# Expert gates scattered into DRAM by accumulating DMAs in place of one-hot matmuls

## The chip, the core and the metric

The kernel runs on one NeuronCore of a Trainium2 chip. The metric is the time of one execution on the device in microseconds (us), of which lower is better. Five engines work side by side and wait for one another on semaphores: TensorE (PE in the profile; PEld is its weight loading), VectorE (DVE), ScalarE (ACT), GpSimd (POOL), and SyncE (SP), which here only issues DMAs. ACT and POOL issue DMAs too.

## The reference

A decoder trunk of two layers over 256 tokens of width 1024 in float32. Each layer adds three things to the residual x: a mixer (stick-breaking attention and retention), a cross-attention to a memory, and PEER, a feed-forward part over 16,384 experts of one neuron each. The change is in PEER, which picks 16 experts for each token and head:

```python
def peer_ffn(h, w_pq, sub_keys, expert_u, expert_v):
    q = (h @ w_pq).reshape(B, S, PEER_HEADS, 2, PEER_DQ // 2)       # 8 heads, 2 halves
    scores = jnp.einsum('bshpd,hpkd->bshpk', q, sub_keys)           # 128 keys per half
    top_s, top_i = lax.top_k(scores, K)                             # K = 16
    cand_s = (top_s[..., 0, :, None] + top_s[..., 1, None, :]).reshape(B, S, PEER_HEADS, K * K)
    cand_i = (top_i[..., 0, :, None] * NK + top_i[..., 1, None, :]).reshape(B, S, PEER_HEADS, K * K)
    best_s, best_pos = lax.top_k(cand_s, K)
    expert_idx = jnp.take_along_axis(cand_i, best_pos, axis=-1)
    gate = jax.nn.softmax(best_s, axis=-1)
    ...
        a = jnp.einsum('cd,chkd->chk', hc, u)                       # u, v: rows expert_idx
        w = gc * jax.nn.gelu(a, approximate=False)
        return jnp.einsum('chk,chkd->cd', w, v)
```

The kernel computes this densely: the product of h with all 16,384 rows of expert_u, a gelu, a product with a dense gate matrix G (expert by token, zero where an expert was not picked), and the product with all rows of expert_v.

## The kernel before

All weights stream through SBUF in 680 units of 512 KB in the order of their use (`Stream`, L31 to L69): SP loads a unit into one of three `raw` buffers (L48), ACT rounds it to `hi` (L57), and DVE forms the rest `lo` (L59); three pairs of `hi` and `lo` exist, so that two units are ready ahead of the one that PE works on. SP carries out its list in order, and the load of a unit waits there until the `raw` buffer of three units before is free, that is until its `lo` is done. A unit's product takes three matmuls for each pair of tiles (`hi`·hi, `hi`·lo, `lo`·hi).

A layer has 84 units for mixer, cross-attention and the query projection `pq` (16 of them), 128 for expert_u and 128 for expert_v. Other work is cut into generators that run one step for each unit (`Side`, L87); `paced` (L72) lets the selection of experts spend a fixed cost per unit, its `rate`, where a step's cost is written beside its `yield`.

In PEER, `stage1` (L796) multiplies queries by keys, `top16` (L784) takes the best 16 on DVE in five instructions, `select` (L821) does this once more over the 256 sums of a head and makes gates and expert numbers for 128 tokens, and transposes them. `g_build` (L893) then makes G in SBUF: for four tokens at a time DVE writes one-hot tiles `oh2` and `oh1` in float16 (L907, L911), PE multiplies them in eight matmuls of 128x128 into `gps` (L900), and ACT copies them into `gt` (L901). That takes 64 steps per layer, beside the units of expert_u.

The gelu of an expert_u product is stored to the DRAM tensor `tdr` as long as G is not complete (L946); afterwards it is multiplied into `gt` at once (`ev_u`, L942). In the expert_v part `w_load` (L967) brings stored gelus back, `w_prep` (L973) multiplies them by `gt` and splits the product into `wh` and `wl`, and `v_mm` (L994) accumulates in `out` (L999). The order of expert_v's units puts the direct ones first.

Of the kernel before, what the change touches and what calls it, by code (L numbers as in the profile page):

```python
# [10 lines left out]
F32 = mybir.dt.float32  # L11
# [4 lines left out]
OP = mybir.AluOpType  # L16
# [10 lines left out]
RATE = 1.12, 1.6  # L27
GS = 2.0 ** 14  # keeps the low parts of small gates clear of float16's smallest numbers
# [43 lines left out]
def paced(g, rate):  # L72
    """spreads g over the units, rate[0] of its cost to each; g yields the cost of a step, None to end a unit's share"""
    credit = 0.0
    while True:
        credit += rate[0]
# [38 lines left out]
def build(tc, ctx, a):  # L115
# [9 lines left out]
    v_at = []  # L125
    for l in range(L):
# [11 lines left out]
        v_at.append(len(units))  # L138
        units += [None] * 128
# [10 lines left out]
    cm = const.tile([128, 256 + 16], F32)  # L150
    gains = const.tile([128, L, 40], F32)
    c_sp = ExitStack()
# [12 lines left out]
    iota = cm[:, 128:256]  # L165
    iota16 = cm[:, 256:272]
    mhalf = const.tile([128, 8], F32)
    G.memset(mhalf, -0.5)
    hT = const.tile([128, KT, 512], F32R)
    tdr = dram.tile([64, 128, 512], F32)  # L170
# [47 lines left out]
    def b_pair_halves(src, evac, mid):  # L218
        """the first pair of such tiles, k = 0-3 of both before mid() and k = 4-7"""
# [18 lines left out]
    def b_units(src, n, evac, first=0):  # L238
        """pairs of [128 n, 256 t] = W^T @ src; evac(pair, psum [128, 2, 256])."""
# [20 lines left out]
    def split_g(src, dst, k0, gain, new_ps):  # L260
        """transposes [128 t, 128] pieces src(tt, 0), src(tt, 1), times gain, into dst[:, k0:k0+2] as hi and lo."""
# [10 lines left out]
    def split_gs(srcs, dst, k0, gain, new_ps):  # L272
        """the same of srcs[tt][:, 0:512], a pair per step"""
# [8 lines left out]
    class Norm:  # L282
        """rmsnorm of x: x is transposed at once, in pieces, times the gain; its 1/rms goes onto the products."""
# [35 lines left out]
    def normed_t(src, gain, dst, hn, new_ps):  # L319
        """dst = transposed rmsnorm(src) * gain, hi and lo"""  # L320
# [27 lines left out]
    for l in range(L):  # L348
# [24 lines left out]
        side.add(load_task())  # L373
        ntri, mask, mneg = (cx[:, i * 128:(i + 1) * 128] for i in range(3))
# [379 lines left out]
        c_pe, c_g0, c_top, c_g1, c_ps = (ExitStack() for _ in range(5))  # L754
        pe = pool(c_pe, "pe", 2)
        slot = pe.tile([128, 2, 4, 128], F16, name="slot")
        iota_x = pe.tile([128, 128, 4], F16, name="slot")
        G.tensor_copy(iota_x, iota[:, :, None].to_broadcast([128, 128, 4]))
        gt = {}
# [12 lines left out]
        def h_task():  # L772
            """the normalized hT of the expert products"""
# [18 lines left out]
        queue = [deque(), deque()]  # L792
        qts = deque()

        def stage1(g, qT):
# [3 lines left out]
            s = pw.tile([128, 2, 128], F32, name="s", bufs=14)  # L799
            A.copy(s, ps)  # L800
            for tt in range(2):
                queue[tt].append(lambda tt=tt: top16(s[:, tt], 128, tv[:, tt, g], ti[:, tt, g]))

        def ev_q(i, ps):
            q2 = pw.tile([128, 2, 256], F32, name="q2")
            A.copy(q2, ps)
            for c in range(2):
                qts.append((2 * i + c, q2[:, c]))

        cands = {}  # L810

        def cand(tt, h):
            if h >= PH or (tt, h) in cands:
                return
            cd = pw.tile([128, TOPK, TOPK], F32, name="cd", bufs=3)
            G.tensor_tensor(cd, tv[:, tt, 2 * h][:, :, None].to_broadcast([128, TOPK, TOPK]),
                            tv[:, tt, 2 * h + 1][:, None, :].to_broadcast([128, TOPK, TOPK]), op=OP.add)
            cands[tt, h] = cd

        def select(tt):  # L820
            """best 16 of the 256 sums per head, gates, expert numbers"""  # L821
            bv = keys.tile([128, PH, TOPK], F32, name="bv", bufs=2)
            bp = keys.tile([128, PH, TOPK], U32, name="bp", bufs=2)
            cand(tt, 0)
            cand(tt, 1)
            yield 0
            for h in range(PH):
                cand(tt, h + 2)
                top16(cands[tt, h].rearrange("p a b -> p (a b)"), 256, bv[:, h], bp[:, h])
                yield 1.7  # L830
            gs = keys.tile([128, 4, PH, TOPK], F32, name="gs", bufs=2)
            be = keys.tile([128, PH, TOPK], F32, name="be", bufs=2)
            V.tensor_tensor(be, bv, bv[:, :, 0:1].to_broadcast([128, PH, TOPK]), op=OP.subtract)
            A.activation(be, be, AF.Exp, scale=rx[:, tt:tt + 1])
            pf = keys.tile([128, 2, PH, TOPK], F16, name="pf", bufs=2)
            for w in range(2):
                pi = keys.tile([128, PH, TOPK], U32, name="pi", bufs=2)
                if w == 0:
                    V.tensor_scalar(pi, bp, 4, None, op0=OP.logical_shift_right)
                else:  # L840
                    V.tensor_scalar(pi, bp, 15, None, op0=OP.bitwise_and)
                V.tensor_copy(pf[:, w], pi)
            yield 1.0
            yield None
            s8 = small.tile([128, PH], F32, name="r8")
            V.tensor_reduce(s8, be, axis=AX.X, op=OP.add)
            V.reciprocal(s8, s8)
            V.tensor_scalar(s8, s8, GS, None, op0=OP.mult)
            V.tensor_tensor(be, be, s8[:, :, None].to_broadcast([128, PH, TOPK]), op=OP.mult)
            g16 = keys.tile([128, PH, TOPK], F16, name="g16")  # L850
            V.tensor_copy(g16, be)
            V.tensor_copy(gs[:, 2], g16)
            V.tensor_sub(gs[:, 3], be, gs[:, 2])
            yield 1.2
            tih = ti[:, tt].rearrange("p (h w) c -> p h w c", w=2)
            for w in range(2):
                for hf in range(2):
                    hs = slice(4 * hf, 4 * hf + 4)
                    tx = keys.tile([128, 4, TOPK, TOPK], F16, name="tx", bufs=2)
                    A.copy(tx, tih[:, hs, w][:, :, :, None].to_broadcast([128, 4, TOPK, TOPK]))  # L860
                    eq = keys.tile([128, 4, TOPK, TOPK], F16, name="eq", bufs=2)
                    V.tensor_tensor(eq, iota16x[:, None].to_broadcast([128, 4, TOPK, TOPK]),
                                    pf[:, w, hs, None, :].to_broadcast([128, 4, TOPK, TOPK]), op=OP.is_equal)
                    yield 0.6
                    V.tensor_mul(eq, eq, tx)
                    yield 0.6
                    V.tensor_add(eq[:, :, 0:8], eq[:, :, 0:8], eq[:, :, 8:16])
                    V.tensor_reduce(gs[:, w, hs], eq[:, :, 0:8].rearrange("p h c s -> p h s c"), axis=AX.X, op=OP.add)
                    yield 0.9
            yield None  # L870
            ps = sps.tile([128, 4, 128], F32, name="sps")
            for w in range(4):
                T.transpose(ps[:, w], gs[:, w].rearrange("p h c -> p (h c)"), ident)
            yield None
            A.copy(slot[:, tt], ps)
            yield 0

        def q_task():
            n = 0
            while n < 32:  # L880
                if qts:
                    for _ in range(2):
                        stage1(*qts.popleft())
                qn = queue[0] if len(queue[0]) >= len(queue[1]) or n >= 24 and queue[0] else queue[1]
                if qn:
                    qn.popleft()()
                    n += 1
                    yield 1.05
                else:
                    yield None  # L890

# [241 lines left out]
```

## Time and profile before

| what | value |
|---|---|
| median of 3 runs | 2158.88 us (2157.48 to 2158.95) |
| span of the profiled execution | 2156.0 us |
| PE busy | 2137.1 us, 99% |
| DVE, ACT, POOL busy | 72%, 54%, 4% |
| granted TensorE clock | 0.999 of full speed (2.4 GHz) |
| DMA | 425.72 MB, 197 GB/s mean |

The span is the time from the first instruction to the last of the one execution that was profiled. The profile gives no other time for that execution; the median of the runs lies 2.9 us above its span. Matmuls are pipelined and their durations overlap, so a matmul's mean in nanoseconds is longer than the step from one to the next: the step is read from starts.

### The profile page before, as it was taken

To read this page: it belongs to the slowest core of one execution; us is meant where nothing else is said; L and a number is where in the kernel's file an instruction comes from. 1 tells how busy PE (TensorE), PEld (TensorE's weight loads), DVE (VectorE), ACT (ScalarE), POOL (GpSimd) and SP (SyncE) were. 2 spreads that over 40 slices of the span, in tenths; PEclk is the share of its full clock that TensorE was granted. 3 is DMA by queue.
4 is the path that set the end of the run, shared out by engine and by line. 5 is a ranking of instruction groups with operands and counts; after the bars stand their busy time and mean duration, and the time that the engine had idled before them with its cause. 6 is when DMAs were issued, how large, how long until landed. Compare 5 with 4: busy or idle time off the path is not lost.

```text
span 2156.0 us, 35478 instructions
## 1 busy us (share of the span) xinstructions
PE 2137.1 (99%) x14028; PEld 1955.8 (91%) x14028; DVE 1544.2 (72%) x2583; ACT 1173.0 (54%) x1483; POOL 81.8 (4%) x87
## 2 busy tenths in 40 slices
PE   8999999999999999999999999999999999999998
PEld 7899899999999988888888899999999998888887
DVE  5775699886766567677676747998876755666776
ACT  6645554556665444444466445545666654444444
POOL 0120000000000000000011100000000000000000
PEclk9999999999999999999999999999999999999999
DMA  6544557775555577777755445677755565777775
GB/s 220 157 152 150 160 177 229 232 231 161 157 162 181 185 234 239 242 243 239 233 183 162 142 151 167 184 236 227 219 162 158 162 184 183 240 240 242 244 244 185
DMA packets 133222, 425.72 MB, mean 197 GB/s; under 512 B 14912, under 2 KB 15040, under 8 KB 132800
## 3 DMA queue, kind: packets, MB, share of 16 engines
q1 hardware_dynamic: 114624, 386.98, 56.5%
q10 hardware_dynamic: 18432, 36.50, 5.8%
q8 instruction: 109, 1.79, 0.3%
q14 instruction: 57, 0.47, 0.1%
HBM read 393.53 MB, written 29.88 MB: 196 GB/s over the span
## 4 chain that ended last, share of the span: by engine, by line
PE 67%; issue 31%; ACT 1%; DVE 1%; DMA 0%; POOL 0%; POOLq 0%; ACTq 0%
PE out L999 16%; PE mm L249 11%; PE mm L250 11%; PE mm L252 11%; PE mm L192 4%; PE mm L194 4%; PE mm L193 4%; PE gps L900 3%; PE sps L798 1%; PE att L689 1%; PE att L720 1%; PE att L425 0%; PE tp L265 0%; PE mm L492 0%; PE mm L228 0%
## 5 line engine op out<-in xcount | busy, mean ns | idle before, releaser
L59 DVE TENSOR_TENSOR lo<-raw,hi 128x1024 fp32r<-128x1024 f32 x680 | 834.2, 1229 | 319.0 <-ACT hi L57 315.6
L57 ACT CAST hi<-raw 128x1024 fp32r<-128x1024 f32 x680 | 713.2, 1051 | 448.1 <-PE mm L250 260.0
L249 PE MATMUL mm<-hT,hi 128*128 128x256 f32 x2272 | 561.9, 286 | 0.0
L250 PE MATMUL mm<-hT,hi 128*128 128x256 f32 x2272 | 552.0, 281 | 0.0
L999 PE MATMUL out<-hi,oh 128*128 128x512 f32 x2048 | 548.9, 389 | 0.0
L999 PEld LDWEIGHTS out<-hi,oh 128*128 128x128 f32 x2048 | 384.3, 188 | 79.5
L249 PEld LDWEIGHTS mm<-hT,hi 128*128 128x128 f32 x2272 | 429.8, 189 | 0.4
L250 PEld LDWEIGHTS mm<-hT,hi 128*128 128x128 f32 x2272 | 428.8, 189 | 0.2
L999 PE MATMUL out<-lo,oh 128*128 128x512 f32 x1024 | 316.7, 389 | 0.0
L252 PE MATMUL mm<-hT,lo 128*128 128x256 f32 x2272 | 315.8, 282 | 0.0
L252 PEld LDWEIGHTS mm<-hT,lo 128*128 128x128 f32 x2272 | 289.3, 188 | 0.0
L999 PEld LDWEIGHTS out<-lo,oh 128*128 128x128 f32 x1024 | 192.3, 188 | 39.8
L901 ACT ACTIVATE gt<-gps 128x512 f32<-128x512 f32 x128 | 137.6, 1113 | 83.2 <-PE gps L900 83.2
L907 DVE TENSOR_TENSOR oh<-slot 128x1024 f16<-128x1024 f16 x128 | 88.3, 690 | 107.5 <-PE gps L900 107.5
L900 PE MATMUL gps<-oh,oh 128*128 128x128 f16 x1024 | 137.4, 297 | 0.0
L900 PEld LDWEIGHTS <-oh 128*128 128x128 f16 x1024 | 107.5, 118 | 6.0
L911 DVE TENSOR_TENSOR oh<-oh,slot 128x1024 f16<-128x1024 f16 x128 | 88.3, 690 | 3.3
L192 PE MATMUL mm<-hi,hT 128*128 128x512 f32 x160 | 64.5, 403 | 0.0
L258 POOL TENSOR_TENSOR rstd<-rstd,mhalf 128x2 f32<-128x2 f32 (+1 forms) x8 | 5.5, 684 | 1550.3 <-DVE rstd L298 1550.3
L194 PE MATMUL mm<-lo,hT 128*128 128x512 f32 x160 | 63.2, 395 | 0.0
L193 PE MATMUL mm<-hi,hT 128*128 128x512 f32 x160 | 63.1, 395 | 0.0
L249 PE MATMUL mm<-hTp,hi 128*128 128x256 f32 x224 | 55.5, 286 | 0.0
(728 smaller groups left out, 2184.0 us busy)
## 6 DMA issues: line engine op xcount, KB each, us to landing
raw<-u SPq DMA_DIRECT2D x256, 512.0 KB, 4.0
raw<-v SPq DMA_DIRECT2D x256, 512.0 KB, 3.6
raw<-w_in_a SPq DMA_DIRECT2D x40, 512.0 KB, 3.5
raw<-pq SPq DMA_DIRECT2D x32, 512.0 KB, 3.4
raw<-w_in_b SPq DMA_DIRECT2D x16, 512.0 KB, 4.8
raw<-wkv_b SPq DMA_DIRECT2D x16, 512.0 KB, 3.6
raw<-w_out SPq DMA_DIRECT2D x16, 512.0 KB, 3.5
raw<-wkv_a SPq DMA_DIRECT2D x16, 512.0 KB, 4.0
```

Source lines behind the costliest of these rows:

```text
L57: self.nc.scalar.copy(hi, r)
L59: self.nc.vector.tensor_sub(lo, r, hi.bitcast(F32))
L192: T.matmul(ps[tt], sh, h3[:, kk], start=(k == 0), stop=False)
L193: T.matmul(ps[tt], sl, h3[:, kk], start=False, stop=False)
L194: T.matmul(ps[tt], sh, l3[:, kk], start=False, stop=(k == KT - 1))
L249: T.matmul(o, h3[:, k], src[:, k, 0:256], start=(k == 0), stop=False)
L250: T.matmul(o, h3[:, k], src[:, k, 256:512], start=False, stop=False)
L252: T.matmul(o, l3[:, k], src[:, k, 0:256], start=False, stop=(k == KT - 1))
L900: T.matmul(ps[:, i], a0[:, 1, :, i], b0[:, w, :, i], start=(w == 0), stop=(w == 1))
L901: pend.append(lambda: A.activation(gt[tt][:, :, c0:c0 + 4].rearrange("p i t -> p t i"), ps, AF.Copy, scale=1.0 / GS))
L907: V.tensor_tensor(a1, iota_x[:, None].to_broadcast([128, 2, 128, 4]), slot[:, tt, 0:2, None, c_].to_broadcast([128, 2, 128, 4]), op=OP.is_ ...
L999: T.matmul(out[tt][dd], st_, mv_[:, dd * 512:(dd + 1) * 512], start=(i == 0 and first), stop=(i == 127 and mv_ is lo))
```

## The change

The one-hot tiles, their matmuls, `gt`, `tdr` and the two orders of expert_v go. In their place stands a DRAM tensor `gd` for each layer and half of the tokens, 16,384 x 128 floats. `zero_task` fills it with zeros from SBUF in 64 DMAs of 256 KB per layer, one per weight unit from the fifth on, on SP's queue. The selection runs in four groups of two heads, each for all 256 tokens. `gates` computes for every gate its place in `gd` (expert number times 128 plus token) and adds the gate there with an indirect accumulating DMA from GpSimd's queue, 128 elements of 4 bytes each: 2 halves x 16 ranks x 8 heads = 256 DMAs per layer. The first DMAs of a head wait until those of the head before have landed. The sums of candidates `cd` move from POOL to DVE. Gelus stay in SBUF (`act0`, `act1`). In the expert_v part SP loads the gates of two units (`gw`, 2 DMAs of 128 KB), and DVE multiplies them by `act`; the very first of these loads waits for all scatter DMAs.

```diff
@@ build
-        units += [None] * 128
+        units += [a["v"][l, i] for i in range(128)]
+    zeros = const.tile([128, 128], F32)
+    gd = [[dram.tile([NK * NK * 128, 1], F32, name=f"gd{l}{tt}") for tt in range(2)] for l in range(L)]
@@ layer
+        def zero_task():
+            for tt in range(2):
+                g_ = gd[l][tt].rearrange("(n p q t) o -> n p q (t o)", p=128, q=4, t=128)
+                for n in range(32):
+                    nc.sync.dma_start(g_[n], zeros[:, None].to_broadcast([128, 4, 128]))
+                    yield
+        side.later(zero_task(), 4)
@@ gates, in place of the end of select and g_build
+                    eq = keys.tile(SH4, F16, name="eq", bufs=2)
+                    V.tensor_tensor(eq, iota16x[:, None].to_broadcast(SH4),
+                                    pf[:, w, tt, :, None, :].to_broadcast(SH4), op=OP.is_equal)
+                    V.tensor_mul(eq, eq, tx[w][tt])
...
-                        T.matmul(ps[:, i], a0[:, 1, :, i], b0[:, w, :, i], start=(w == 0), stop=(w == 1))
-                pend.append(lambda: A.activation(gt[tt][:, :, c0:c0 + 4].rearrange("p i t -> p t i"), ps,
-                                                 AF.Copy, scale=1.0 / GS))
...
+            V.tensor_scalar(gi, ex[:, 0], 128.0, pcol, op0=OP.mult, op1=OP.add)
+            for h in range(HG):
+                now = [[], []]
+                for c in range(TOPK):
+                    for tt in range(2):
+                        i_ = G.indirect_dma_start(
+                            gd[l][tt], bass.IndirectOffsetOnAxis(ap=gi[:, tt, h, c:c + 1], axis=0),
+                            gv[:, tt, h, c:c + 1], None, compute_op=OP.add).ins
+                        for j_ in now[tt]:
+                            tc.declare_no_dep(i_, j_, reason="one head's experts differ")
+                        if c == 0:
+                            for j_ in late[tt]:
+                                tc.add_manual_dep(i_, j_.name, SYNC, reason="the sums of an earlier head")
+                        now[tt].append(i_)
+                late[:] = now
@@ peer_task: four groups; costs 1.6 and 2.6, rate 1.6
+                    for tt in range(2):
+                        top16(sc[k][:, tt], 128, tv[:, tt, k], ti[:, tt, k])
+                        yield 1.6
...
+                        V.tensor_tensor(cd, tv[:, tt, 2 * h][:, :, None].to_broadcast([128, TOPK, TOPK]),
+                                        tv[:, tt, 2 * h + 1][:, None, :].to_broadcast([128, TOPK, TOPK]), op=OP.add)
+                        top16(cd.rearrange("p a b -> p (a b)"), 256, bv[:, tt, h], bp[:, tt, h])
+                        yield 2.6
+                yield from gates(slice(hs.start, hs.stop))
@@ ev_u, w_load, w_prep
+            A.activation(act[i // 32][:, i % 32], ps, AF.Gelu)
...
+                tw[n] = gw = pe.tile([128, 2, 256], F32, name="gw")
+                for tt in range(2):
+                    g_ = gd[l][tt].rearrange("(n c p t) o -> n p c (t o)", c=2, p=128, t=128)
+                    i_ = nc.sync.dma_start(gw[:, :, tt * 128:tt * 128 + 128], g_[n]).ins
+                    if n == 0:
+                        for j_ in late[tt]:
+                            tc.add_manual_dep(i_, j_.name, SYNC, reason="all gates")
...
+                V.tensor_mul(gw, gw, act[n // 32][:, n % 32])
```

On PE, in the middle of the first layer's expert_u part, this stands before (a unit's last matmuls, eight one-hot matmuls of which one is shown, the next unit):

```order
L249 MATMUL mm_5459<-hT_93,hi_5359 128x256
L250 MATMUL mm_5459<-hT_93,hi_5359 128x256
L252 MATMUL mm_5459<-hT_93,lo_5361 128x256 x8
L900 LDWEIGHTS oh2_5442
L900 MATMUL gps_5494<-oh1_5444,oh2_5442 128x128
...
L249 MATMUL mm_5459<-hT_93,hi_5397 128x256
L250 MATMUL mm_5459<-hT_93,hi_5397 128x256
```

and this now at the same place:

```order
L251 MATMUL mm_6150<-hT_93,hi_6089 128x256
L252 MATMUL mm_6150<-hT_93,hi_6089 128x256
L254 MATMUL mm_6150<-hT_93,lo_6091 128x256 x8
L251 MATMUL mm_6150<-hT_93,hi_6120 128x256
L252 MATMUL mm_6150<-hT_93,hi_6120 128x256
```

The units follow one another with nothing between them.

On POOL, this followed the layer's last 1/rms (`rstd`) before, in the selection:

```order
L758 CAST slot_2421<-cm_75 128x512 [waits DMAHW4_49,DMAHW3_49,DMAHW7_49,PE_49,Activation_49]
L768 CAST iota16x_2438<-cm_75 128x256 [waits Pool_49]
L816 TENSOR_TENSOR cd_3718<-tv_2435 128x256 [waits DVE_49]
L816 TENSOR_TENSOR cd_3720<-tv_2435 128x256 [waits DVE_49]
L816 TENSOR_TENSOR cd_3722<-tv_2435 128x256 [waits DVE_49]
L816 TENSOR_TENSOR cd_3794<-tv_2435 128x256 [waits DVE_49,Pool_49]
```

and this stands there now (DMASW0 to DMASW7 are eight semaphores on which the scatter DMAs tell that they have landed):

```order
L774 CAST iota16x_2504<-cm_75 128x256 [waits DMAHW4_49,DMAHW3_49,DMAHW7_49,PE_49,Activation_49]
L865 DMA gd00_96<-gv_3188,gi_3189 2097152x1 [waits DMAHW3_49,DMAHW5_49,DMAHW1_49,DMAHW7_49,DVE_49,Activation_49]
L865 DMA gd01_97<-gv_3188,gi_3189 2097152x1 [waits DMAHW4_49,DMAHW3_49,DMAHW5_49,DMAHW2_49,DMAHW6_49,DMAHW1_49,DMAHW7_49,DMAHW0_49,Activation_49]
L865 DMA gd00_96<-gv_3188,gi_3189 2097152x1
...
L865 DMA gd00_96<-gv_3188,gi_3189 2097152x1 [waits DMASW0_49]
L865 DMA gd01_97<-gv_3188,gi_3189 2097152x1 [waits DMASW1_49]
L865 DMA gd00_96<-gv_3188,gi_3189 2097152x1 [waits DMASW2_49]
```

The 16 additions `cd` of a layer left POOL; 256 DMAs came, and each from the ninth on waits for the one eight before it.

On SP, where the loads of expert_v begin in the first layer, this stood before:

```order
L48 DMA raw_8233<-u 128x1024 [waits DMAHW2_49,DVE_49]
L48 DMA raw_8264<-u 128x1024 [waits DMAHW3_49,DVE_49]
L48 DMA raw_8298<-v 128x1024 [waits DMAHW4_49,DVE_49]
L48 DMA raw_8329<-v 128x1024 [waits DMAHW5_49,DVE_49]
L48 DMA raw_8363<-v 128x1024 [waits DMAHW6_49,DVE_49]
```

and this stands there now:

```order
L48 DMA raw_7798<-v 128x1024 [waits DMAHW1_49,DVE_49]
L923 DMA gw_7825<-gd00_96 128x2x128 [waits DMASW2_49,DMASW4_49,DMASW0_49,DMASW6_49,PE_49,Pool_49]
L923 DMA gw_7825<-gd01_97 128x2x128 [waits DMASW5_49,DMASW7_49,DMASW3_49,DMASW1_49]
L923 DMA gw_7828<-gd00_96 128x2x128
L923 DMA gw_7828<-gd01_97 128x2x128
L923 DMA gw_7845<-gd00_96 128x2x128 [waits DMAHW6_49,DMAHW5_49,DVE_49]
L923 DMA gw_7845<-gd01_97 128x2x128 [waits DMAHW2_49]
L48 DMA raw_7857<-v 128x1024 [waits DMAHW3_49,DVE_49]
```

The loads of gates stand in SP's list between those of the weights, the first two behind a wait for the scatter DMAs.

## Rows read from the trace of the kernel before

**Rows 1.** The page, its head and part 1: busy time of each engine.

```profile
span 2156.0 us, 35478 instructions
...
PE 2137.1 (99%) x14028; PEld 1955.8 (91%) x14028; DVE 1544.2 (72%) x2583; ACT 1173.0 (54%) x1483; POOL 81.8 (4%) x87
```

**Rows 2.** The page, part 4: the chain that ended last, by engine and line.

```profile
PE 67%; issue 31%; ACT 1%; DVE 1%; DMA 0%; POOL 0%; POOLq 0%; ACTq 0%
PE out L999 16%; PE mm L249 11%; PE mm L250 11%; PE mm L252 11%; PE mm L192 4%; PE mm L194 4%; PE mm L193 4%; PE gps L900 3%; PE sps L798 1%; PE att L689 1%; PE att L720 1%; PE att L425 0%; PE tp L265 0%; PE mm L492 0%; PE mm L228 0%
```

**Rows 3.** Five stretches of layer one: busy us and instructions, clock, DMA, GB/s.

```profile
22.00:266.00 244.00, 243.33 (x1479) 216.93 (x1478) 160.41 (x247) 135.60 (x205) 27.80 (x22) 1.00 0.52 165
...
308.00:350.00 42.00, 42.00 (x357) 42.00 (x356) 40.39 (x143) 21.01 (x25) 0.00 (x0) 1.00 0.78 233
...
410.00:450.00 40.00, 40.00 (x340) 40.00 (x338) 35.13 (x84) 21.17 (x25) 3.11 (x5) 1.00 0.74 233
...
500.00:680.00 180.00, 180.00 (x1518) 177.21 (x1517) 126.41 (x158) 117.63 (x124) 0.00 (x0) 1.00 0.55 162
680.00:722.00 42.00, 42.00 (x357) 42.00 (x356) 21.86 (x28) 19.95 (x24) 0.00 (x0) 1.00 0.59 184
```

**Rows 4.** The chain in order of time, layer two: start us, length us, what.

```profile
1387.10 0.95 PE mm L252 x8
1401.34 0.95 PE mm L252 x8
...
1555.06 0.96 PE gps L900 x8
```

**Rows 5.** Line L900: duration ns min/median/max, first and last start.

```profile
L900 PE MATMUL gps<-oh,oh x1024: 285/297/303, 481.4 to 1748.6; 128*128 128x128 f16 x171
```

**Rows 6.** Timeline of DVE in the selection: start us, length us, instruction.

```profile
321.12 0.29 DVE L785 MAX8 tv<-s 128x8 f32<-128x128 f32 x1
...
322.70 1.21 DVE L59 TENSOR_TENSOR lo<-raw,hi 128x1024 fp32r<-128x1024 f32 x1
323.82 0.29 DVE L785 MAX8 tv<-s 128x8 f32<-128x128 f32 x1
...
416.49 0.42 DVE L785 MAX8 bv<-cd 128x8 f32<-128x256 f32 x1
...
418.74 0.41 DVE L785 MAX8 bv<-cd 128x8 f32<-128x256 f32 x1
```

**Rows 7.** Groups of DVE by line: count, busy us, mean ns, idle before.

```profile
L991 DVE TENSOR_TENSOR oh<-gt,oh 128x256 fp32r<-128x256 f32 x36 | 13.7, 421 | 18.1 <-ACT oh L990 18.1
...
L862 DVE TENSOR_TENSOR eq<-iota16x,pf 128x1024 f16<-128x1024 f16 x16 | 11.0, 685 | 0.0
```

**Rows 8.** Groups of POOL by line, in the same columns.

```profile
L816 POOL TENSOR_TENSOR cd<-tv 128x256 f32<-128x256 f32 x32 | 19.9, 621 | 326.7 <-DVE mr L788 262.0 <-DVE tv L789 64.7
L528 POOL TENSOR_TENSOR rotk<-w,w 128x256 f32<-128x256 f32 x4 | 6.9, 1724 | 0.0
...
L258 POOL TENSOR_TENSOR rstd<-rstd,mhalf 128x2 f32<-128x2 f32 (+1 forms) x8 | 5.5, 684 | 1550.3 <-DVE rstd L298 1550.3
```

**Rows 9.** DMA: a queue's packets, MB and share; us to landing; SP's issue ns.

```profile
q1 hardware_dynamic: 114624, 386.98, 56.5%
...
raw<-u SPq DMA_DIRECT2D x256, 512.0 KB, 4.0
...
L48 SPq DMA_DIRECT2D raw<-u x256: 327/328/328, 291.1 to 1784.5; - x128
```

**Rows 10.** Timeline where expert_v begins, and line L984's cast.

```profile
727.77 1.22 DVE L59 TENSOR_TENSOR lo<-raw,hi 128x1024 fp32r<-128x1024 f32 x1 [0.96 <-ACT hi L57]
...
730.27 1.08 PE L999 MATMUL out<-hi,oh 128*128 128x512 f32 x4
...
731.83 0.76 DVE L991 TENSOR_TENSOR oh<-gt,oh 128x256 fp32r<-128x256 f32 x2
...
L984 ACT CAST oh<-tt__8767 x1: 624/624/624, 774.0 to 774.0; 128x512 fp32r<-128x512 f32 x1
```

More of the change, by code (lines that the diff above doesn't have):

```diff
@@ L26 @@
 NEG = -1e30
[L27 to L28 removed]
+RATE = 1.6
+GROUPS = 4
 class Stream:
@@ L75, in paced @@
     while True:
-        credit += rate[0]
+        credit += rate
         while credit > 0:
@@ L798, in stage1 @@
                 T.matmul(ps[:, tt], qT[:, tt * 128:(tt + 1) * 128], kt[:, g], start=True, stop=True)
[L799 to L802, printed above, removed]
+            sc[g] = pw.tile([128, 2, 128], F32, name="s", bufs=14)
+            A.copy(sc[g], ps)
         def ev_q(i, ps):
@@ L820, in select @@
[L820 to L835, printed above, removed]
+        bv = keys.tile([128, 2, PH, TOPK], F32, name="bv")
@@ new lines, in build, with gates @@
+        bp = keys.tile([128, 2, PH, TOPK], U32, name="bp")
+        HG = PH // GROUPS
+        SH = [128, 2, HG, TOPK]
+        SH4 = [128, HG, TOPK, TOPK]
+        late = [[], []]
+        def gates(hs):
+            gv = pe.tile(SH, F32, name="gv", bufs=GROUPS)
+            gi = pe.tile(SH, U32, name="gi", bufs=GROUPS)
+            b_ = bv[:, :, hs]
+            V.tensor_tensor(gv, b_, b_[:, :, :, 0:1].to_broadcast(SH), op=OP.subtract)
+            for tt in range(2):
+                A.activation(gv[:, tt], gv[:, tt], AF.Exp, scale=rx[:, tt:tt + 1])
+            tih = ti.rearrange("p a (h w) c -> p a h w c", w=2)
+            ex = keys.tile([128, 2, 2, HG, TOPK], F32, name="ex", bufs=2)
+            pf = keys.tile([128, 2, 2, HG, TOPK], F16, name="pf", bufs=2)
+            tx = [[keys.tile(SH4, F16, name="tx", bufs=4) for _ in range(2)] for _ in range(2)]
@@ L870, in select @@
[L870 to L890, printed above, removed]
@@ L920, in build @@
-        direct = []
-        order = []
-        def peer_task():
-            yield from q_task()
-            yield from select(0)
-            yield from select(1)
-            gt[0] = pool(c_g0, "gp0", side="right").tile([128, 128, 128], F32, name="gt0")
-            c_top.close()
-            gt[1] = pool(c_g1, "gp1").tile([128, 128, 128], F32, name="gt1")
-            rate[0] = RATE[1]
-            yield from g_build()
-            yield None
-            yield None
-            direct.append(True)
@@ new lines, in gates @@
+            yield 0.8
+        def peer_task():
+            for g in range(GROUPS):
+                hs = range(HG * g, HG * g + HG)
+                for k in range(2 * HG * g, 2 * HG * g + 2 * HG):
+                    while k not in sc:
+                        if qts:
+                            stage1(*qts.popleft())
+                        else:
+                            yield None
+                    for tt in range(2):
+                        top16(sc[k][:, tt], 128, tv[:, tt, k], ti[:, tt, k])
+                        yield 1.6
+                for h in hs:
+                    for tt in range(2):
+                        cd = pw.tile([128, TOPK, TOPK], F32, name="cd")
+                        V.tensor_tensor(cd, tv[:, tt, 2 * h][:, :, None].to_broadcast([128, TOPK, TOPK]),
[3 more added lines that the diff above has]
+                yield from gates(slice(hs.start, hs.stop))
@@ L940, in build @@
         c_mix.close()
+        act = [pool(c_g0, "act0", side="right").tile([128, 32, 2, 256], F32, name="act0"), None]
         def ev_u(i, ps):
-            if not direct:
-                t = pe.tile([128, 512], F32, name="tt_")
-                A.activation(t, ps.rearrange("p a t -> p (a t)"), AF.Gelu)
-                nc.sync.dma_start(tdr[i], t)
-                order.append(i)
-                return
-            if direct == [True]:
-                direct.append(i)
-                late = list(range(i, 64))
-                es = late + [j for j in range(64) if j < i]
-                order[:] = es
-                for n, j in enumerate(es):
-                    for c in range(2):
-                        units[v_at[l] + 2 * n + c] = a["v"][l, 2 * j + c]
@@ L957, in ev_u, with to_last @@
-            t = pe.tile([128, 2, 256], F32, name="tt_")
-            A.activation(t, ps, AF.Gelu)
-            for tt in range(2):
-                g_ = gt[tt][:, 2 * i:2 * i + 2]
-                V.tensor_mul(g_, g_, t[:, :, tt * 128:(tt + 1) * 128])
-        b_units(hT, 128, ev_u)
-        assert not t_p in side.tasks
-        i_dir = direct[1]
+            A.activation(act[i // 32][:, i % 32], ps, AF.Gelu)
+        def to_last():
+            side.drain(t_p)
+            c_top.close()
+            act[1] = pool(c_g1, "act1").tile([128, 32, 2, 256], F32, name="act1")
@@ L1021, in build @@
             nx = Norm(None, None, ps_of(mm, "mm"), None)
-            gf = [pe.tile([128, 512], F32, name="slot") for b in range(2)]
+            g2 = st.raw_pool.tile([128, 1024], F32, name="raw")
+            gf = [g2[:, b * 512:b * 512 + 512] for b in range(2)]
             for b in range(2):
@@ L1027, in build @@
         w = tw.pop(63)
-        last = [st.get(), st.get(1)]
         xg = {}
```

138 lines of the change are left out of this document (40 added, 98 removed).

## The prediction

> **What bounds the kernel now.** I read the page's busy shares first, then the chain, then the PEER stretches. PE is busy 99% of the span and nothing else exceeds 72% [rows 1]. The chain is PE work and "issue", time with no wait behind it [rows 2]; DMA, ACT and DVE together hold about 2%. In the stretches PE is full in each of the PEER ones, at full clock, while the other engines change [rows 3]. So a matmul that goes is worth its step on PE, and anything put in its place costs nothing until something makes PE wait.
>
> The reader should see two prices on PE. Five units of expert_u without one-hot matmuls take 1401.34 - 1387.10 = 14.24 us, 2.85 each; eight one-hot matmuls hold the chain for another 0.96 [rows 4]. The 297 ns of one such matmul [rows 5] is its pipelined length, eight of which would be 2.38: it overlaps its neighbours and is not the price.
>
> **What goes.** 64 steps of eight matmuls in two layers, 1024 in all [rows 5], are 128 x 0.955 = 122.2 us, all on PE and on the end's path. The 16 transposes of `select` go too: at the same 0.12 a piece, 2 us. The DVE, ACT and POOL work that vanishes with them (`oh`, `gt`, `cd`) lay beside PE and gives nothing back itself.
>
> **The selection on DVE.** It now costs 1.6 per unit in the schedule. Measured: a top16 over 128 runs from 321.12 to 322.70, 1.58 us, and `lo` takes 1.12 to the next start; one over 256 takes 418.74 - 416.49 = 2.25 [rows 6]. The `cd` that DVE takes over has 128x256 elements, as the product in L991 with 421 ns [rows 7], so 2.25 + 0.42 = 2.67 against the 2.6 written. The smaller `eq` of 512 elements should take about half of L862's 685 ns [rows 7], 0.34, and 0.68 for two against 0.7 written. So DVE needs about 1.12 + 1.6 = 2.72 of a unit's 2.85: full, but PE still sets the pace, as it did where DVE was busy 40.39 of 42 us [rows 3]. Cost 0, bounded by the DVE rival below.
>
> **Zero filling.** 64 DMAs of 256 KB per layer are 16.8 MB between weight loads, and SP spends 0.33 us on an issue [rows 9]. The weight queue moved 387 MB in 56.5% of the span [rows 9], that is 387 / (0.565 x 2156) = 0.318 MB per us of full DMA use, so a layer's zeros need 53 us of it if 512-byte pieces go as fast as the weights' long ones. They fall in a stretch of 244 us with a DMA share of 0.52 [rows 3]: 0.52 + 53/244 = 0.74, a share that other stretches carry with PE full (0.78 [rows 3]). Cost 0, covered by the three raw buffers. If that cover were gone and all of it stalled, 2 x 53 = 106.
>
> **The scatter DMAs.** This decides. Per layer there are 256 on POOL's queue. In DVE's new order 123 units lie between the indices of the first group and the first product with gates, 123 x 2.85 = 350 us; the groups become ready 19 or 20 units (55 us) apart, and the last is ready 65 units (185 us) before the product. If one DMA occupies POOL for G, and each head's barrier adds the landing of the head before (a weight load lands 4.0 us after issue [rows 9], about 3 of it not covered by POOL's work, 8 times: 24), the scatter ends in time as long as 256 G + 24 < 350, G < 1.27 us.
>
> No row shows a DMA on POOL. From below: SP's issue, 0.33 us [rows 9], hidden. From above: each waits for its own landing, 4.0 us, and 2 x (256 x 4.0 - 326) = 1396 us are added. Between lie POOL's own operations: 0.62 and 0.68 for the short ones, 1.72 for a long one [rows 8]. Eight DMAs may be open at once, so the landing of one holds the ninth only if it exceeds 8 G. I take the middle of POOL's rows, (0.62 + 1.72) / 2 = 1.17: 256 x 1.17 + 24 = 324, hidden with 26 us to spare. That is thin.
>
> The Trainium skill (DMA: Bandwidth & Descriptors, Anatomy of one DMA — SWDGE (gpsimd) path) gives a fit of about 2.0 us plus bytes for each DMA of GpSimd, and says that most of it is the receipt of the write. Taken as time in which POOL is held, it would give 2 x (512 - 326) = 372 us more; taken as a latency that eight open DMAs share, it changes nothing. No run here shows which.
>
> **The start of expert_v.** `w_load` stands in SP's list behind the weight load that waits for the `lo` of 727.77, which ends at 728.99 [rows 10]. Three issues of 0.33 follow, the gates land 4.0 us after the last of them starts [rows 9], at about 733.7, and product (0.7), cast (0.62) and difference (0.76) [rows 10] make it 735.8. PE could start at 730.27 [rows 10]: 5.6 us of waiting per layer, 11.2 in all. Before, the first gates were in SBUF and PE waited for nothing there. SP's next weight loads stand behind the third gate load, which waits for the first difference; three raw buffers are filled by then, so no second wait. From there DVE does one product of 512 elements where it did two of 256, PE sets the pace, and the gate loads replace loads of the same size.
>
> **Sum.** Profiled execution: span 2156.0 - 122.2 - 2.0 + 11.2 = 2043.0. The runs' median lay 2.9 above the span, so 2046 us, 5.2% less.
>
> **The rivals.**
>
> A. The scatter is too slow, and the end of expert_u waits for it: slower. POOL's list is one line, the first gate load waits for all of it, and the weight loads stand behind that load in SP's list, so PE runs dry two units later. Per layer the lateness is 256 G - 326. At G = 1.72, the rate of POOL's long operation [rows 8], 114 us, twice 114 = 229, time 2275. It outweighs the 113 net gain from G = (326 + 56.5) / 256 = 1.49 on. For it: 128 elements with addresses of their own are no short job, and DVE is full beside it. Against: most of POOL's short rows lie near 0.7.
>
> The skill's 2.0 us as a rate belongs here: 2046 + 372 = 2418.
>
> B. The scatter is late, but by less than it saves: G between 1.27 and 1.49. At 1.38, 2 x 27 = 54, time 2100.
>
> C. DVE becomes the bound. It has 0.13 us of slack per unit. If each `lo` waits for half a short POOL operation, 0.31, while DMAs are being issued, the 58 units from the first group to the last lose 58 x 0.18 = 10 per layer, 2067; at a whole one, 0.62, 28 per layer, 2103. The trace hardly tests it: in the selection POOL was busy for 3.11 of 40 us and PE stayed full [rows 3], whereas now POOL would work most of the time.
>
> The Trainium skill (SBUF — State Buffer, Who interferes with whom) says that a DVE instruction with two inputs in SBUF contends with a GpSimd instruction that reads SBUF; `lo` is one. No run here shows it yet.
>
> D. The small pieces hold up the weight stream, zeros in the mixer or 4-byte additions beside expert_u. Bound by the zeros' 106: 2152 at most, where half of that, 2099, is already more than the buffers should let through.
>
> **How the numbers follow.** The forecast has 0.53, A 0.26, B 0.13, C 0.05, D 0.03. The likeliest case by itself lies between 2030 (no wait at expert_v, 11, and 5 for small waits that vanish) and 2075 (20 us of DVE or scatter waits, and 9 more at the stages' edges). The range reaches from 2030 to 2200: B, C and D fall inside, and A up to G = 1.58; above it I leave 0.18, below it 0.02. Two measurements of this kernel that differ by less than 0.2% can't be told apart. Within that bound lies only a strip of A, 0.02. Faster 0.74, slower 0.24.
>
> **What would show each step.** PE's step from unit to unit in expert_u should be 2.85 from the first to the last, and no `gps` products. POOL's queue should show 512 DMAs; the mean step from one to the next in a group, counted without the barriers, is G, and decides between forecast, B and A. The last scatter DMA of a layer should land before the last unit of expert_u ends; if it does not, SP's wait before the first `gw` load is the loss, and PE's idle time at `out` has the same length. PE should wait 5 to 6 us at the first `out` of each layer. `lo` at 1.23 us beside the scatter speaks against C, a longer one or gaps in PE during the selection for it. In the mixer PE's busy share should stay as it was; if `hi` waits for `raw` there, D was right. I am wrong if G exceeds 1.27, or if the weights come late.

## The result: 15% slower, and the profile after

The changed kernel takes 2485.5 us (median of 4 runs, 2481.5 to 2489.5) against 2158.8: the ratio is 1.152, with a 95% interval of 1.150 to 1.153. The forecast was 2046, with a range from 2030 to 2200. Of the profiled execution of the kernel after, the page shows this, the counterpart of [rows 1, 2]:

```profile
span 2484.1 us, 34167 instructions
...
PE 2028.2 (82%) x12988; PEld 1851.5 (75%) x12988; DVE 1397.4 (56%) x2309; ACT 1043.6 (42%) x1365; POOL 1019.4 (41%) x566
...
PE 55%; issue 19%; POOL 17%; DVE 6%; ACT 2%; DMA 1%; POOLq 0%; SPq 0%; ACTq 0%
...
L865 POOL DMA_INDIRECT gd<-gv,gi x512 | 960.1, 1875 | 299.4 <-issue 152.9
```

PE's busy time did fall, by 109 us, and yet the span grew by 328. POOL, at 4% before, is now in the chain with 17%, all of it on one line, the scatter DMA. 960 us of POOL for 512 DMAs are 1.88 us each.

The stretches of layer one, in the columns of [rows 3] (busy us of PE, PE's loads, DVE, ACT and POOL, the granted clock, DMA share, GB/s):

```profile
22.00:266.00 244.00, 242.17 (x1473) 216.50 (x1472) 159.70 (x241) 135.07 (x204) 26.19 (x20) 1.00 0.78 235
...
410.00:450.00 40.00, 38.69 (x322) 38.28 (x320) 35.81 (x98) 22.10 (x29) 34.21 (x20) 1.00 0.71 169
500.00:660.00 160.00, 160.00 (x1336) 160.00 (x1335) 69.65 (x57) 73.84 (x86) 140.59 (x59) 1.00 0.71 189
680.00:880.00 200.00, 0.00 (x0) 0.00 (x0) 0.00 (x0) 0.00 (x0) 167.09 (x108) 0.50 0.23 0
892.00:900.00 8.00, 8.00 (x24) 6.30 (x25) 4.87 (x6) 2.61 (x3) 0.00 (x0) 0.65 0.31 103
900.00:1000.00 100.00, 100.00 (x443) 82.84 (x442) 68.55 (x74) 48.83 (x56) 0.00 (x0) 1.00 0.76 240
```

The reader should see the fourth row first. For 200 us nothing runs on the core but POOL, 108 DMAs in a row, and not a byte of weights moves. From the rows above it the cause can already be read: while PE still works, POOL gets through only 59 DMAs in 160 us, 2.7 us each.

Who waits for whom at that place, in the waits of the kernel after (us in total, times, longest), and in the timeline at its end (start us, length us, instruction, idle time before it):

```profile
DVE gw L931 <- DMA gw<-gd: 442.9, 25, 216.2
...
PEld out L943 <- ACT wh L934: 432.3, 2, 216.3
...
POOL gd L865 <- issue: 152.9, 500, 0.4
...
POOL gd L865 <- DMA gd<-gv,gi: 9.3, 5, 2.8
```

```profile
884.81 1.55 POOL L865 DMA_INDIRECT gd<-gv,gi  x1 [0.30 <-issue]
...
890.45 0.69 DVE L931 TENSOR_TENSOR gw<-gw,act 128x512 f32<-128x512 f32 x1 [215.88 <-DMA gw<-gd]
891.18 0.62 ACT L934 CAST wh<-gw 128x512 fp32r<-128x512 f32 x1 [214.47 <-DVE gw L931]
...
891.85 1.22 PE L943 MATMUL out<-hi,wh 128*128 128x512 f32 x2 [215.78 <-ACT wh L934]
```

Two waits of 216 us, one per layer, are more than the whole loss of 328. The first product of expert_v waits for the cast, that for the product with the gates, that for the first gate load, and that for the last scatter DMA, which ends at 886.4. POOL itself was held by the landing of earlier DMAs for 9.3 us in all: it was working.

SP's own waits show why no weights move meanwhile. Its list stands at the first gate loads (L923), and the weight loads come behind them:

```profile
SPq L923 <- DMA gd<-gv,gi: 425.4, 8, 203.9
```

By stages, each from its first matmul: expert_u took 372.5 and 371.5 us where it took 427.2 twice (-110.4), the waits are 216.1 and 216.4 (+432.5), expert_v took 351.7 and 350.8 for 348.9 and 347.9 (+5.6), the second mixer -1.0, start and tail +1.4: together +328.1, as the spans differ.

### The profile page after: what moved, and what is told of

The parts are those of the page before. It is cut to its first block, busy times and chain, and to the rows that moved or that the text cites. A ratio compares the mean times of both kernels' runs of the same rounds, so it can differ in the third digit from the quotient of the medians.

```text
span 2484.1 us, 34167 instructions
## 1 busy us (share of the span) xinstructions
PE 2028.2 (82%) x12988; PEld 1851.5 (75%) x12988; DVE 1397.4 (56%) x2309; ACT 1043.6 (42%) x1365; POOL 1019.4 (41%) x566
## 4 chain that ended last, share of the span: by engine, by line
PE 55%; issue 19%; POOL 17%; DVE 6%; ACT 2%; DMA 1%; POOLq 0%; SPq 0%; ACTq 0%
POOL gd L865 17%; PE out L943 14%; PE mm L251 9%; PE mm L252 9%; PE mm L254 9%; PE mm L194 3%; PE mm L195 3%; PE mm L196 3%; DVE lo L59 3%; ACT hi L57 1%; PE sps L804 1%; PE att L699 1%; PE att L730 1%; DMA gd<-zeros 0%; DVE mr L794 0%
## 5 line engine op out<-in xcount | busy, mean ns | idle before, releaser
L865 POOL DMA_INDIRECT gd<-gv,gi x512 | 960.1, 1875 | 299.4 <-issue 152.9
L943 PE MATMUL out<-hi,wh 128*128 128x512 f32 x1024 | 319.2, 392 | 431.9 <-ACT wh L934 431.9
L943 PEld LDWEIGHTS out<-hi,wh 128*128 128x128 f32 x1024 | 193.6, 189 | 472.4 <-ACT wh L934 432.3
L934 ACT CAST wh<-gw 128x512 fp32r<-128x512 f32 x128 | 79.7, 623 | 700.8 <-DVE gw L931 512.5
L931 DVE TENSOR_TENSOR gw<-gw,act 128x512 f32<-128x512 f32 x128 | 87.9, 687 | 444.0 <-DMA gw<-gd 442.9
L943 PE MATMUL out<-hi,wl 128*128 128x512 f32 x1024 | 318.4, 391 | 0.0
L943 PE MATMUL out<-lo,wh 128*128 128x512 f32 x1024 | 318.2, 391 | 0.0
L943 PEld LDWEIGHTS out<-hi,wl 128*128 128x128 f32 x1024 | 193.4, 189 | 40.6 <-DVE wl L935 0.4
L943 PEld LDWEIGHTS out<-lo,wh 128*128 128x128 f32 x1024 | 193.4, 189 | 40.4
L935 DVE TENSOR_TENSOR wl<-gw,wh 128x512 fp32r<-128x512 f32 x128 | 88.6, 692 | 106.2 <-ACT wh L934 106.2
```

The costliest lines, as they stand in the source:

```text
L865: i_ = G.indirect_dma_start(gd[l][tt], bass.IndirectOffsetOnAxis(ap=gi[:, tt, h, c:c + 1], axis=0), gv[:, tt, h, c:c + 1], None, compute_o ...
L931: V.tensor_mul(gw, gw, act[n // 32][:, n % 32])
L934: A.copy(wh, gw)
L935: V.tensor_sub(wl, gw, wh.bitcast(F32))
L943: T.matmul(out[tt][dd], st_, mv_[:, dd * 512:(dd + 1) * 512], start=(i == 0 and first), stop=(i == 127 and mv_ is lo))
```

## The experiments

Theory 1: POOL is busy with each scatter DMA for 1.55 us and 0.30 us more pass until it starts the next; where a VectorE operation with both inputs in SBUF is running at the start, the DMA is held until that operation ends. 256 of them take longer than expert_u. Rivals: the landing of the DMAs, the traffic of the weights, or the selection itself sets the pace.

**Half of the scatter DMAs.**

```diff
-                for c in range(TOPK):
+                for c in range(0, TOPK, 2):
```

> Leaves out every second of the 16 ranks of each head: 128 scatter DMAs per layer instead of 256, all else as in the kernel after (half of the gates are missing). Theory 1 (POOL takes 1.55 to 2.6 us for each DMA, and only the length of its queue holds the output products up): 128 DMAs at 2.2 to 2.6 us are 282 to 333 us, or the selection's own pace, so the last is done before the 352 us between the first scatter and the end of expert_u; TensorE's wait of 216 us per layer falls to some 6 to 11 us, and the time to 2485.5 - 2 x 205 to 210 = 2065 to 2076 us. Rival (each DMA waits for a landing, or the selection itself is what comes late, at its own pace): the last DMA still ends after expert_u, the wait stays above 50 us per layer and the time above 2150 us.

Measured: 2060.9 us, ratio to the kernel before 0.956 (0.954 to 0.957). The last of layer one's 128 DMAs in the timeline, and PE's waits in both layers together:

```profile
635.51 2.58 POOL L865 DMA_INDIRECT gd<-gv,gi  x1 [0.30 <-issue]
```

```profile
PE out L943 <- ACT wh L934: 9.4, 2, 5.1
```

It ends at 638.1, 37 us before expert_u does, and PE's wait falls from 216 to 5 us. The time is 4 us below the range that I gave, which had taken the wait as at least 6. On this point Theory 1 holds: the length of the queue decides.

**No scatter DMAs at all.**

```diff
-            for h in range(HG):
-                now = [[], []]
...
-                late[:] = now
```

> All scatter DMAs are left out (no gates at all), everything else is as in the kernel after. What is left is the rest of the prediction's sum: 2046 us by it. With half of the scatter DMAs it was 2061 us, and 0.03 us more in each weight unit is most of the difference. Theory (a program with scatter DMAs on POOL has the longer unit everywhere): 2.85 us per unit here, 2061 - 10 = 2051 us. Rival (the longer unit has another cause, and hidden scatter DMAs cost nothing): 2.88 us per unit, 2058 to 2063 us.

Measured: 2061.9 us, ratio 0.956 (0.954 to 0.957), the same as with 128 per layer. So scatter DMAs that are covered cost nothing, POOL's use and the additions in DRAM included, and the rest of my sum is measured by itself: 2062 where it said 2046. (The zeros are still written in both kernels; what they cost is read from the mixer, below.) The waits of this kernel in both layers, and its stretches in layer one:

```profile
PEld out L929 <- ACT wh L920: 10.9, 2, 5.7
```

```profile
410.00:450.00 40.00, 38.79 (x322) 38.39 (x321) 35.68 (x98) 22.03 (x29) 0.00 (x0) 1.00 0.51 171
...
681.00:689.00 8.00, 7.59 (x24) 6.03 (x25) 5.04 (x6) 2.97 (x4) 0.00 (x0) 0.70 0.30 98
690.00:790.00 100.00, 100.00 (x443) 82.81 (x442) 69.78 (x74) 48.65 (x56) 0.00 (x0) 1.00 0.76 243
```

The start of expert_v costs 5.5 us per layer, as forecast (5.6). What the sum missed is small: PE idles 1.2 us in the first of these stretches, in the selection, with no DMA on POOL, where it was full before [rows 3]; and after the wait of 5 us the clock is at half speed for some us (24 matmuls in 8 us, where 35 are usual).

**No subtraction on VectorE beside the scatter** (`plain` is set over expert_u alone).

```diff
+            if self.plain:
+                self.nc.scalar.copy(lo, r)
+            else:
                 self.nc.vector.tensor_sub(lo, r, hi.bitcast(F32))
```

> In expert_u alone ScalarE copies the weight into lo in place of VectorE's subtraction (leaves out the subtraction, so lo isn't the low part); all 256 scatter DMAs are issued. Theory 1 (a two-input VectorE operation holds up a scatter DMA that starts beside it): without the 128 subtractions per layer nearly all DMAs take 1.55 us and follow each other at 1.86 us, but for those beside the selection's VectorE work; 256 x 1.86 to 1.95 = 476 to 500 us, the last ends 64 to 88 us earlier per layer, time 2485.5 - 128 to 176 = 2310 to 2358 us. Rival (the weight stream's DMA traffic slows POOL, which goes on beside expert_u just the same): heads 0 to 4 stay at 2.2 to 2.8 us per DMA, time 2480 to 2490 us.

Measured: 2317.3 us (one run, as for the next two experiments). The queue of this kernel, and of the kernel after in the same place:

```profile
565.50 1.55 POOL L869 DMA_INDIRECT gd<-gv,gi  x1 [0.30 <-issue]
567.36 1.55 POOL L869 DMA_INDIRECT gd<-gv,gi  x1 [0.30 <-issue]
569.21 1.55 POOL L869 DMA_INDIRECT gd<-gv,gi  x1 [0.30 <-issue]
571.07 1.55 POOL L869 DMA_INDIRECT gd<-gv,gi  x1 [0.30 <-issue]
```

```profile
566.87 2.57 POOL L865 DMA_INDIRECT gd<-gv,gi  x1 [0.30 <-issue]
569.75 2.58 POOL L865 DMA_INDIRECT gd<-gv,gi  x1 [0.30 <-issue]
...
566.79 1.23 DVE L59 TENSOR_TENSOR lo<-raw,hi 128x1024 fp32r<-128x1024 f32 x1 [1.65 <-ACT hi L57]
569.67 1.23 DVE L59 TENSOR_TENSOR lo<-raw,hi 128x1024 fp32r<-128x1024 f32 x1 [1.65 <-ACT hi L57]
```

This is the reading that settles it. In the kernel after, a DMA starts at 566.87, 0.08 us into a `lo` that ends at 568.02, and it ends at 569.44, 1.42 later. Over all 210 DMAs of that run that start within a `lo`, the median time from its end to the DMA's end is 1.43 (1.41 to 1.43 from the tenth to the ninetieth percentile); three that start together with the `lo` keep 1.55. The next DMA starts 0.31 later, again just into a `lo`: the queue locks to the unit, one DMA per 2.88 us (43 of the 57 steps from 500 to 660 us). Without the subtraction nearly all take 1.55 (512 DMAs, mean 1.550). The stretches of that kernel:

```profile
410.00:450.00 40.00, 40.00 (x336) 40.00 (x335) 18.18 (x79) 34.45 (x44) 31.07 (x21) 1.00 0.73 175
500.00:660.00 160.00, 160.00 (x1335) 160.00 (x1335) 0.00 (x0) 125.46 (x139) 128.11 (x83) 1.00 0.74 183
```

From 500 to 660 us VectorE does nothing and POOL gets through 83 DMAs instead of 59, with nearly the same traffic (183 GB/s, 189 in the kernel after), so the traffic is out as a rival. `lo` itself takes 1.23 as before the change: DVE is not held, POOL is. The first line answers another question: with VectorE relieved, PE is full in the selection, so the 1.2 us that it idled there without scatter DMAs were VectorE's own load. But 256 x 1.86 = 476 us still exceed expert_u, and PE waits 138 and 132 us.

**A copy on VectorE instead,** in the same place.

```diff
+                self.nc.vector.tensor_copy(lo, r)
```

> In expert_u alone VectorE makes lo by a copy of the weight, one input from SBUF instead of two (leaves out the subtraction); all 256 scatter DMAs are issued. If it is the second input that holds POOL up: DMAs of 1.55 us at 1.86 us, time as without VectorE, 2310 to 2358 us. If any VectorE operation of this size holds it up: some DMAs still stretch by up to the copy's duration, step 2.0 to 2.9 us, time 2400 to 2490 us. If it is the DMA traffic: 2480 to 2490 us.

Measured: 2344.3 us, within the range for "only the second input", but the trace says otherwise:

```profile
561.59 1.71 POOL L869 DMA_INDIRECT gd<-gv,gi  x1 [0.30 <-issue]
563.61 1.55 POOL L869 DMA_INDIRECT gd<-gv,gi  x1 [0.30 <-issue]
...
561.18 0.69 DVE L61 CAST lo<-raw 128x1024 fp32r<-128x1024 f32 x1 [2.18 <-PE mm L258]
```

A DMA that starts within the copy waits for its end too: 101 of them in both layers, in the median 1.42 us from the copy's end to theirs. So two inputs are not the condition, and there Theory 1 was too narrow. It costs less because the copy is shorter, 0.69 for 1.23, and fewer DMAs start within one (101, with `lo` 210). Here VectorE is not quite untouched: of 223 copies that start while a DMA is being issued, 17 take 0.80 to 1.04 us. My two cases did not separate by time; the single rows do.

**Half of the tokens in each DMA.**

```diff
-                            gd[l][tt], bass.IndirectOffsetOnAxis(ap=gi[:, tt, h, c:c + 1], axis=0),
-                            gv[:, tt, h, c:c + 1], None, compute_op=OP.add).ins
+                            gd[l][tt], bass.IndirectOffsetOnAxis(ap=gi[0:64, tt, h, c:c + 1], axis=0),
+                            gv[0:64, tt, h, c:c + 1], None, compute_op=OP.add).ins
```

> Each scatter DMA carries the gates of 64 of its 128 tokens (leaves out the other 64), the number of DMAs stays 256 per layer. If POOL's 1.55 us are paid per element: some 0.8 us plus the 0.30 us gap, 256 x 1.1 to 1.9 = 282 to 486 us, TensorE's wait falls to 10 to 140 us per layer, time 2065 to 2330 us. If they are paid per DMA: 1.5 us as before, time 2470 to 2490 us. My own guess is between them: half fixed, 1.15 us, and 0.30 us, with the VectorE waits 256 x 1.8 = 460 us, time about 2280 us.

Measured: 2347.2 us. POOL's times in this run and in the kernel after (ns, min/median/max):

```profile
L865 POOL DMA_INDIRECT gd<-gv,gi x512: 1391/1404/2407, 324.1 to 1980.3; - x171
```

```profile
L865 POOL DMA_INDIRECT gd<-gv,gi x512: 1538/1555/2633, 322.3 to 2116.9; - x171
```

64 elements less save 0.15 us of 1.55: most of the price is per DMA, by a straight line through these two points (an estimate) about 1.25 us, and 2.4 ns per element. My guess (1.15 us) took half of it as fixed; too little. The total fell by 138 us all the same. By an estimate from the mean steps about half of that is the shorter DMA itself. The rest comes from the steps beside expert_u: this DMA no longer locks to the unit there, and the mean step falls from 2.47 to 2.04, by 0.43 where the shorter DMA gives 0.15.

**Half and half.** The second 128 tokens go by scatter, the first 128 keep the one-hot matmuls, in 32 steps instead of 64.

```diff
-            for t4 in range(64):
+            for t4 in range(32):
...
+                for c in range(TOPK):
+                    i_ = G.indirect_dma_start(
+                        gd[l], bass.IndirectOffsetOnAxis(ap=gi[:, h, c:c + 1], axis=0),
+                        gv[:, h, c:c + 1], None, compute_op=OP.add).ins
+                    ...
+                    G.memset(nop, 0.0)
```

> Half and half: the gates of the second 128 tokens go by scatter DMAs (128 per layer, selected first, in four groups of heads, with a memset of one column between two DMAs on POOL), those of the first 128 stay with the one-hot matmuls (32 of 64 groups per layer); gelu of the units that are multiplied late goes through DRAM as in the kernel before; constants 280 columns wide. Theory 1: 128 DMAs at 2.2 to 2.6 us from about 315 us end at 600 to 650 us, before expert_u, which takes 365 + 30 = 395 us from 303 us; the time is 2158.8 - 61.1 (half of the one-hot matmuls) - 1 (transposes) + 2 x 5.5 (start of the output products) + 2 x 5 (places where VectorE is full during the selection) = 2118 us. Rival (selection of one half after the other and the one-hot work that comes behind it end later than expert_u, or VectorE becomes its bound): TensorE waits at the end of expert_u, over 2140 us.

Measured: 2142.0 us, ratio to before 0.9927 (0.9914 to 0.9941), a small gain of 0.7% with 1 outside the interval, and 0.86 of the kernel after by the medians. The last DMAs end at 599.7 and 1652.5, more than 100 us before expert_u, and PE waits 2.8 and 3.7 us where expert_v begins. It misses its forecast by 24 us, most of it here, the output products of this kernel and those of the kernel after (ns, min/median/max):

```profile
L1074 PE MATMUL out<-hi,oh x2048: 390/396/796, 706.2 to 2132.1; 128*128 128x512 f32 x187
```

```profile
L943 PE MATMUL out<-hi,wh x1024: 389/389/797, 891.9 to 2474.4; 128*128 128x512 f32 x171
```

From start to start these are 0.2333 and 0.2267 us: 2 x 1536 x 0.0066 = 20 us.

**Where the few ns per matmul come from.** In the kernel after and in all its variants a unit of expert_u takes 2.880 us without scatter DMAs beside it too, before 2.848; that is 8 us of the 16 by which the rest of the sum was short. Six kernels asked whether it is where the tiles lie or that scatter DMAs exist. The edits: `cm` 280 columns wide (with half of the DMAs); `cm` 276 wide in the kernel before; the zeros allocated ahead of `x` (with half of the DMAs); a tile of 512 bytes behind `hT` in the kernel before; one scatter DMA in the kernel before; and for the half-and-half kernel the zeros ahead of `x` and `nop` 64 bytes wide.

```diff
-    cm = const.tile([128, 256 + 16 + 4], F32)
+    cm = const.tile([128, 256 + 16 + 8], F32)
...
+    zeros = const.tile([128, 128], F32)
     x = const.tile([128, 2, D], F32)
...
+    G.indirect_dma_start(one_d, bass.IndirectOffsetOnAxis(ap=one_i[:, 0:1], axis=0), one[:, 1:2], None, compute_op=OP.add)
```

> As the kernel with half of the scatter DMAs (leaves out every second rank's gates), and the tile of constants is 280 columns wide instead of 276, so that the tiles behind it start at a multiple of 32 bytes as they did with 272. Theory (the 2.88 us of a unit in expert_u, 2.85 before, come from that start address): a unit at 2.85 us again, 128 x 0.032 = 4 us less per layer, time 2060.9 - 8 = 2053 us. Rival (the 0.03 us come from something else of the change, a longer queue on an engine or the DMA traffic): 2.88 us, time 2059 to 2063 us.

> The kernel before with its tile of constants 276 columns wide instead of 272 and nothing else. By the same theory its units of expert_u and of the other weight stretches that read hT slow from 2.85 to 2.88 us: at least 8 us more, 2167 us. Rival: no change, 2157 to 2160 us.

> As the kernel with half of the scatter DMAs (leaves out every second rank's gates), and the 512 bytes of zeros lie ahead of x instead of behind hT, so that hT and the tiles of the weight stream have the distance from each other that they had before the change. Theory (the distance between the moving and the stationary tile sets the 2.85 or 2.88 us of a unit): 2.85 us in every unit that reads hT, about 190 units per layer and 0.03 us each, 2061 - 10 = 2051 us. Rival (it is not a matter of where the tiles lie): 2.88 us, 2059 to 2063 us.

> The kernel before with an unused tile of 512 bytes of zeros behind hT and nothing else. By the same theory its units that read hT slow from 2.85 to 2.88 us: 2158 + 8 to 12 = 2166 to 2170 us. Rival: 2156 to 2160 us.

> The half-and-half kernel with two changes of place: the zeros ahead of x, and the tile that the memset between two DMAs writes 64 bytes wide instead of 4, so that the tiles behind it start at a multiple of 64 bytes. Its output matmuls took 0.233 us each where those of before took 0.227. Theory (the 4 bytes set the stationary tiles of the output products off, the zeros the units of expert_u): 0.227 us again, 2 x 1536 x 0.0066 = 20 us less, and 2 x 4 us in expert_u: 2142 - 28 = 2114 us. Rival (the split stage's other work on VectorE and ScalarE, or its DMA traffic, slows the matmuls): 0.233 us, 2134 to 2144 us.

> The kernel before with one scatter DMA of 128 elements more, at its start, into a DRAM tile that nothing reads (and five small instructions that make its row numbers). Theory (the presence of scatter DMAs in the program lengthens every weight unit): 2.88 us in place of 2.85, 2158 + 8 to 12 = 2166 to 2170 us. Rival: 2157 to 2162 us.

Measured, in this order: 2061.2, 2156.8, 2061.7, 2157.3, 2143.8 and 2160.1 us; the rival each time. The median step from unit to unit is 2.880, 2.848, 2.880, 2.848, 2.880 and, with one scatter DMA in the kernel before, 2.840. Neither theory of place holds, nor does the presence of scatter DMAs: with none (above) the unit is 2.880 too. In expert_u the step is nearly the same throughout a program and changes between programs. But the kernel before has units of 2.88 us as well, in its mixer (from 175.6 to 188.7 us), so the step is not set once for a whole program either. Its cause stays open.

## Why the prediction was wrong

The step that failed is the one it named as deciding, the time G of a scatter DMA on POOL. I took 1.17 us, the middle between POOL's short operations and its longest one [rows 8], because no row showed a DMA there. Measured are 2.20 from DMA to DMA on average (564 us for 256 in layer one): 2.47 beside expert_u, 1.86 with nothing beside it. Both lie above the longest POOL row I had, 1.72; ordinary operations of an engine were no bracket for a DMA that it issues. The other side of the comparison was right: I gave the queue 350 us, and from the first DMA (322.3) to the end of expert_u (675.8) there are 353.5. 564 - 353.5 + 5.5 for the way to PE is 216, the wait measured. Seen by its parts, POOL gets through 143 DMAs until expert_u ends, and the 113 that are left take 113 x 1.86 = 210 us alone on the core:

```profile
303.00:675.00 372.00, 369.88 (x3078) 369.14 (x3077) 252.81 (x536) 185.81 (x227) 303.47 (x143) 1.00 0.70 183
```

The mechanism of the rival A was right in every link: the first gate load waits for the whole list, the weights stop behind it, PE runs dry at `out`. That VectorE holds the DMAs beside the weight units was not in it. Its price was too low, 2275, since 1.72 was. The Trainium skill (DMA: Bandwidth & Descriptors, Anatomy of one DMA — SWDGE (gpsimd) path) had about 2.0 us fixed for a DMA of GpSimd, and the estimate by it as a rate, 2418, was the nearest of all; but it puts most of this down to completion, and here POOL itself is busy for 1.55 us and then waits for hardly any landing (9.3 us in all).

Point by point, the rest:

- One-hot matmuls and transposes, -124: expert_u of the kernel without scatter DMAs took 372.6 and 371.2 us, by the sum 427.2 - 62.1 = 365.1. Of the 7.5 and 6.1 us too many, 128 x 0.032 = 4.1 are the longer unit, whose cause is open. Most of the rest is the selection, to which I had given 0 because VectorE would be full but PE would set the pace: with the subtraction taken off VectorE, expert_u took 369.5 twice, 3.1 and 1.7 less.
- Start of expert_v, 5.6 per layer (735.8 - 730.27 is 5.5): measured 5.5, right. The half clock after it was not in the sum: expert_v took 2.2 us more per layer.
- Zero filling, 0: right. The mixer's DMA share rose from 0.52 to 0.78 (forecast 0.74), with PE busy 242.2 of 244 us where it was 243.3, and the second mixer took 1.0 us less than before. With the experiment without scatter DMAs, which leaves out the 4-byte additions, that refutes D.
- C had the two engines the wrong way round. DVE was to wait for POOL; `lo` kept its 1.23 us and POOL waited. The Trainium skill's rule (SBUF — State Buffer, Who interferes with whom), that a VectorE instruction with two inputs in SBUF contends with a GpSimd instruction that reads SBUF, agrees with the trace as far as `lo` goes (the scatter DMA is held for the rest of it). I had weighed the contention for DVE alone, and it cost the queue 0.34 us per DMA instead (2.20 for 1.86). The copy with one input held DMAs as well.
- The 24 us of landings between heads were 9.3 for both layers together.

The range ended at 2200 because A had only 0.26, and that came from the same bracket. The break-even that the prediction worked out was G = 1.49, and its own bounds were 0.33 and 4.0 us. Nothing measured spoke for the lower part; an open term on which the sign hangs needed even chances.

## What to carry to other kernels

Where a change puts many small DMAs on one engine's queue, the count times the engine's time per DMA stands against the time until the first reader; here 256 x 1.86 us did not fit into 353 us even with nothing beside them, 128 did and cost nothing. A price that no row shows is not bounded by other operations of that engine, and if the sign of the result hangs on it, the chances should be even. Such work can be split between the queue and the engine it relieves, up to what the queue can hide; half and half gained 0.7% here.

## What the runs showed of the hardware

- A scatter DMA of 128 four-byte elements holds POOL for 1.55 us, 1.40 with 64 elements, and 0.30 us pass until the next one starts.
- Such a DMA that starts within the two-input `lo` of 128x1024, or within VectorE's copy of 128x1024, takes the rest of that operation and 1.43 us more (1.42 behind the copy). `lo` isn't slowed: beside DMAs it takes 1.26 us at most. The copy mostly isn't: 17 of 223 took 0.80 to 1.04 us instead of 0.70. A DMA that starts before a `lo` keeps its 1.55 us (the median of 83). Beside the weight units the queue locked to them, 2.88 us per DMA.
- After a wait of 216 us the granted clock is at its lower level, 1.2 GHz (0.50 in the stall, 0.65 over the first 8 us of expert_v). In these 8 us 24 matmuls run where 35 are usual, at 0.2267 us each a loss of 2.6 us. After a wait of 5 us the first 8 us show 0.70, and the loss is nearly the same: expert_v as a whole is 2.2 us longer than before, after the long wait 2.8.
- The step of the same matmuls differs from program to program, 2.840 to 2.880 us for a unit of 24 in expert_u, and 0.2267 to 0.2333 us for an output matmul. This is not explained.
